# Filters' loop in another order, token tiles in pairs, a fourth bank, and the filters' norms divided out in the second layer's coefficients

## The chip, the cores and the metric

The kernel runs on 1 core of one Trainium2 chip. The time is that of the device, in microseconds (us), the median of several runs. The engines are TensorE (PE, with its weight loads PEld), VectorE (DVE), ScalarE (ACT), GpSimd (POOL) and SyncE (SP), which issues nearly all DMAs.

## The reference

A backbone of two layers over 1024 tokens of width 1024, with 256 context tokens before them. The first layer is attention of two kinds side by side, the second a gated long convolution ("Hyena") of order 2. What the change touches is the second layer's filters and the way their norm is taken:

```
def hyena_filters(L, w1, b1, w2, b2, w3, b3, freq):
    ...                                  # a small MLP over positions, then a decay
    h = h * jnp.exp(-t * jnp.abs(deltas))[:, None, None, :]
    fwd, bwd = h[:, :, 0], h[:, :, 1]
    kern = jnp.concatenate([fwd, zeros, bwd[:0:-1]], axis=0)
    kern = kern / jnp.sum(jnp.abs(kern), axis=0, keepdims=True)
    return jnp.fft.rfft(kern, axis=0)

def long_conv(u, k_f, skip):
    y = irfft(rfft(u, n=2 * L) * k_f)[:, :L]
    return y + u * skip

    u = short_conv(p[..., :3 * 1024], conv_w, conv_b)     # three taps and a bias
    z = parts[0]
    for o in range(2):
        z = parts[o + 1] * long_conv(z, k_f[:, o], skip[o])
```

The first layer's input is `rms_norm(x, w) * (1 + scale) + shift`, token by token.

## The kernel before

The program has stages: the filters' loop (to about 250 us), the first layer's input projections, attention (480 to 990), output projection, and the second layer's projections and convolutions from about 1090 on. PE, ACT, DVE and POOL work each in the order in which the program is written (`manual_schedule`); SP's order is chosen by the framework.

**The filters' loop** (L615) has 38 iterations n. The steps are pairs of a channel block p of 128 channels (8 of them) and a group gq of taps (4), so 32 steps; the second stage runs six iterations behind. In the order of the program one iteration does: `taps` on PE into a two-bank tile `pw`; `second_stage(.., 0)` on PE into a bank of `pq`; `decayed` (L541), the multiplication of the taps by the decay on DVE; two exponentials of the next step on ACT; `spectra(.., 0)`, which takes the second stage out of its bank on DVE, times the reciprocal norm `rns[p]` (L594), into `kc` and stores it to `Kd` in DRAM; `first_stage` of the step before (PE, then a copy `aT` on ACT), twice, with two more exponentials between; `halves`, a sum and a difference on POOL (L561); `norms`, the sum of absolute values on DVE (L548) and its addition on POOL (L552); `second_stage(.., 1)`; once in four the product `pn` with ones (L649), which sums the norm over the partitions; `regroup`, four DMAs `au<-aT`; `spectra(.., 1)`; once in four the reciprocal of the norm (L661). Once in four also `coefs` (three loads) and `split_coefs` (six ACT copies, two POOL and two DVE subtractions, L345 to L349) for the next block.

**Token tiles.** At the end of an iteration generators are advanced: `modulations` (to n = 6), `row_stats` (to n = 11) and `xprep`, for the first layer's input, from n = 11 on, two `yield`s an iteration from n = 13 to 32. `xprep` takes ten tiles of 128 tokens: it scales one by its rows' norm (L408, DVE), loads the next, and for each half of the width transposes four blocks (L414, PE), scales and shifts them in four ACT instructions (L419) into `mraw`, rounds them (L426, DVE, two casts of 128x256 or one of 128x512) and subtracts (L427, POOL).

**Banks.** `pq` hands out the banks t0, t1, v in turn, and c from n = 20 on. A bank is written again only when what it held was read.

**First weights.** At n = 22 (W1N) the first projection weights `w0` are loaded, at n = 24 split into two parts (four ACT copies L678, four POOL subtractions L679), at n = 26 the next ones loaded; products with them are put at n = 32 to 35 (HP) and behind the loop.

**Second layer.** `tables` loads the convolution's coefficients `cw` (L1750, single elements) and tables FA and IA; `kernel_load` loads `Kd` and the skip row, and adds the skip to the spectrum's real part.

## Time and profile before

| | us |
|---|---|
| median of 3 runs | 1794.36 (1793.38 to 1795.69) |
| the profiled execution | 1791.72 |
| its span, first to last instruction | 1789.9 |
| TensorE busy in the span | 1698.6 (95%) |
| VectorE, GpSimd, ScalarE busy | 1136.4, 837.1, 751.7 |

TensorE's matmuls are pipelined, so that their busy times overlap one another and a busy TensorE is not one at its peak. The share of busy time is a mean over stages with different limits, so it is read stage by stage below. The granted clock is that of TensorE, as a share of 2.4 GHz.

### The profile page before, as it was taken

To read this page: it belongs to the slowest core of one execution; us is meant where nothing else is said; L and a number is where in the kernel's file an instruction comes from. 1 tells how busy PE (TensorE), PEld (TensorE's weight loads), DVE (VectorE), ACT (ScalarE), POOL (GpSimd) and SP (SyncE) were. 2 spreads that over 40 slices of the span, in tenths; PEclk is the share of its full clock that TensorE was granted. 3 is DMA by queue.
4 is the path that set the end of the run, shared out by engine and by line. 5 is a ranking of instruction groups with operands and counts; after the bars stand their busy time and mean duration, and the time that the engine had idled before them with its cause. 6 is when DMAs were issued, how large, how long until landed. Compare 5 with 4: busy or idle time off the path is not lost. (4 is left out here: it accounts for less than half of the span.)

```text
span 1789.9 us, 25447 instructions
## 1 busy us (share of the span) xinstructions
PE 1698.6 (95%) x9360; PEld 1313.9 (73%) x9360; DVE 1136.4 (63%) x1625; ACT 751.7 (42%) x1293; POOL 837.1 (47%) x612
## 2 busy tenths in 40 slices
PE   6888899998999999999999999999999999999898
PEld 2555588986766666666666788888888888878786
DVE  6888957636666665466665324556777667756843
ACT  4766621243545545644444333233333333333331
POOL 3667832524179877677777453123222223233300
PEclk8999999999999999999999999999999999999999
DMA  7776787322220010100010226456776666686432
GB/s 258 243 217 200 211 260 266 110 71 72 57 57 28 11 44 14 52 31 24 22 34 22 78 94 161 138 152 203 199 213 174 196 201 196 196 231 181 155 108 104
DMA packets 237372, 236.48 MB, mean 132 GB/s; under 512 B 30575, under 2 KB 195223, under 8 KB 236831
## 3 DMA queue, kind: packets, MB, share of 16 engines
q1 hardware_dynamic: 235072, 232.76, 43.6%
q10 hardware_dynamic: 2176, 2.10, 0.4%
q8 instruction: 74, 1.21, 0.3%
q14 instruction: 50, 0.41, 0.1%
HBM read 152.87 MB, written 61.94 MB: 120 GB/s over the span
## 5 line engine op out<-in xcount | busy, mean ns | idle before, releaser
L1010 DVE TENSOR_REDUCE mx<-pq 128x1 f32<-128x512 f32 x256 | 170.9, 682 | 100.4 <-PE pq L1009 98.6
L1315 ACT ACTIVATE PT<-pw 128x1024 f32<-128x1024 f32 x160 | 163.6, 1025 | 166.1 <-PE pw L1297 160.1
L100 PE MATMUL pw<-h1h,wh 128*128 128x512 f32 x512 | 208.4, 407 | 0.0
L102 PE MATMUL pw<-h1h,wl 128*128 128x512 f32 x512 | 201.3, 393 | 0.0
L101 PE MATMUL pw<-h1l,wh 128*128 128x512 f32 x512 | 200.0, 391 | 0.0
L1209 POOL TENSOR_TENSOR acc<-acc,PT 128x1024 f32<-128x1024 f32 x62 | 147.4, 2378 | 20.4 <-ACT PT L1315 18.9
L1733 POOL TENSOR_TENSOR wl<-wr,wh 128x1024 fp32r<-128x1024 f32 x32 | 77.1, 2409 | 137.8 <-ACT wh L1732 127.5
L102 PEld LDWEIGHTS pw<-h1h,wl 128*128 128x128 f32 x512 | 96.1, 188 | 21.3
L101 PEld LDWEIGHTS pw<-h1l,wh 128*128 128x128 f32 x512 | 96.5, 188 | 17.7
L100 PEld LDWEIGHTS pw<-h1h,wh 128*128 128x128 f32 x512 | 96.5, 188 | 17.4
L1868 POOL TENSOR_TENSOR K<-K,skp 128x512 f32<-128x512 f32 x32 | 42.7, 1337 | 122.7 <-DMA K<-Kd 121.7
L1207 POOL TENSOR_TENSOR acc<-PT,PT 128x1024 f32<-128x1024 f32 x31 | 74.0, 2386 | 52.5 <-ACT PT L1315 49.8
L1881 DVE TENSOR_TENSOR cA<-pq,K 64x512 f32<-64x512 f32 x128 | 88.1, 689 | 1.8
L1877 DVE SCALAR_TENSOR_TENSOR cB<-pq,K 64x512 f32<-64x512 f32 x64 | 44.4, 693 | 70.4 <-PE pq L1874 35.6
L1848 ACT COPY caT<-pq 128x512 f32<-128x512 f32 x64 | 37.6, 588 | 118.1 <-PE pq L102 98.1
L583 PE MATMUL pq<-au,FBk 128*128 128x256 f32 x256 | 71.6, 408 | 14.8 <-DVE kc L594 11.1
L1894 PEld LDWEIGHTS pq<-cA,GB 128*128 128x128 f32 x512 | 67.3, 193 | 15.3 <-issue 10.3
L1200 PE MATMUL pv<-PT,Va 128*64 128x256 f32 x640 | 77.9, 385 | 0.0
L1896 ACT COPY cbT<-pq 128x512 f32<-128x512 f32 x64 | 37.5, 587 | 95.7 <-PE pq L1894 67.1
L1200 PE MATMUL pv<-PT,Vm 128*64 128x256 f32 x640 | 77.7, 385 | 0.0
L1894 PE MATMUL pq<-cA,GB 128*128 128x128 f32 x512 | 68.8, 278 | 7.9 <-DVE cA L1884 6.9
L1911 DVE TENSOR_TENSOR cil<-spare,cih 128x512 fp32r<-128x512 f32 x64 | 53.8, 879 | 34.8 <-ACT cih L1910 34.6
(448 smaller groups left out, 4672.6 us busy)
## 6 DMA issues: line engine op xcount, KB each, us to landing
au<-aT SPq DMA_DIRECT2D x128, 128.0 KB
space<-in_ada_w_dram SPq DMA_DIRECT2D x32, 512.0 KB
wr<-in_hy_w_in_dram SPq DMA_DIRECT2D x32, 512.0 KB
K<-Kd SPq DMA_DIRECT2D x64, 256.0 KB
ad<-caT SPq DMA_DIRECT2D x64, 256.0 KB
cau<-ad SPq DMA_DIRECT2D x32, 512.0 KB
bd<-cbT SPq DMA_DIRECT2D x32, 512.0 KB
spare<-bd SPq DMA_DIRECT2D x64, 256.0 KB
```

Source lines behind the costliest of these rows:

```text
L100: nc.tensor.matmul(ps, lh, rh, start=start, stop=False)
L101: nc.tensor.matmul(ps, lh, rl, start=False, stop=False)
L102: nc.tensor.matmul(ps, ll, rh, start=False, stop=stop)
L583: nc.tensor.matmul(ps[:, i * CB:(i + 1) * CB], FBk[:, 4 * uc + 2 * j + i, :], aus[p, uc][:, 2 * j + i, :], start=True, stop=True)
L1010: nc.vector.reduce_max(m[:, i, j:j + 1], ps, axis=AX.X)
L1200: nc.tensor.matmul(ps[64 * e:64 * e + 64, 0:256], vals[:, 2 * s + j], PT[:, j, 256 * e:256 * e + 256], start=s == 0 and j == 0, stop=s == ...
L1207: eng.tensor_tensor(accs[gi], prev, PT, ALU.add)
L1209: eng.tensor_tensor(accs[gi], accs[gi], PT, ALU.add)
L1315: nc.scalar.activation(PT, ps.rearrange("p (a q) -> p a q", q=512), AF.Exp, scale=SC_A if kind == 0 else SC_M)
L1733: nc.gpsimd.tensor_tensor(wl, f(r), f(wh), ALU.subtract)
L1881: nc.vector.tensor_tensor(A1[64 * e:64 * e + 64], pv[64 * e:64 * e + 64], K[:, 0], ALU.mult)
L1894: nc.tensor.matmul(ps[:, i * P:(i + 1) * P], GB[:, 4 * uc + i, :], A1[:, i, :], start=True, stop=True)
```

## The change

The second copy of a spectrum goes to ScalarE, and both copies no longer multiply. The norm (not its reciprocal) is copied out of its bank by ScalarE and stored to DRAM (`nd`). In the attention (groups 20 and 22) it is loaded again, with a channel on each partition; the skip row is multiplied by it and stored (`sd`), and its reciprocal is taken; in `tables` the short convolution's coefficients of parts 1 and 2 are multiplied by the reciprocal. The convolution then adds the skip times the norm to the unnormalised spectrum, and the part that multiplies the result carries the division.

Token tiles go in pairs: one activation covers 256 columns, one cast and one subtraction 128x512. The four steps of a pair's quarter (transposes; activations; cast and subtraction; at the end of the pair loads and scaling) stand at four places of an iteration: ahead of the taps, behind the decay multiplication, between `halves` and `norms`, and behind `norms`. Five tiles are loaded at once at n = 11, into the three tiles ckh, ckl, kpe as well. As these hold tokens for longer, the weights' load, split and second load move from n = 22, 24, 26 to 26, 32, 34, and the products from n = 32 to 33. The fourth bank joins at the end of n = 6, not 19.

```diff
-W1N = 22
-HP = {32: 1, 33: 1, 34: 1, 35: 1}
+W1N = 26
+XT = ("xt", "xt") + CK + ("xt", "xt", "ckl", "xt", "kpe")
+LN = 2, 1, 2, 0, 0
+HP = {33: 1, 34: 1, 35: 1, 36: 1}
...
-        load()
+        def scaled(t):
+            for i in range(t, min(t + 2, NC + NT)):
+                nc.vector.tensor_scalar(xts[i], xts[i], rr[:, i:i + 1], 0.0, ALU.mult, ALU.add)
+
+        load(5)
         yield
-        for t in range(NC + NT):
+        scaled(0)
+        yield
+        for t in range(0, NC + NT, 2):
...
+            for k0 in range(0, NK, 2):
+                ps = pq()
+                for k in range(2):
+                    for i in range(2):
+                        nc.tensor.transpose(ps[:, (2 * k + i) * P:(2 * k + i + 1) * P], xts[t + i][:, (k0 + k) * P:(k0 + k + 1) * P], ident)
                 yield
...
+                for k in range(2):
+                    kk = k0 + k
+                    nc.scalar.activation(raw[:, k], ps[:, 256 * k:256 * k + 256], AF.Identity, bias=Sh[:, kk:kk + 1], scale=A[:, kk:kk + 1])
                 yield
...
+                nc.vector.tensor_copy(hi, raw)
+                nc.gpsimd.tensor_tensor(lo, raw, f(hi), ALU.subtract)
+                yield
+                if k0 == NK - 2:
+                    load(LN[t // 2])
+                    scaled(t + 2)
+                yield
...
-            nc.vector.tensor_tensor(kc.rearrange("p h u c -> p u h c"), ps.rearrange("p (u h c) -> p u h c", h=2, c=P),
-                                    rns[p].rearrange("p (h c) -> p h c", c=P).unsqueeze(1).to_broadcast([P, 2, 2, P]), ALU.mult)
+            (nc.vector.tensor_copy, nc.scalar.copy)[j](kc.rearrange("p h u c -> p u h c"), ps.rearrange("p (u h c) -> p u h c", h=2, c=P))
...
+            tokens = 12 < n < 33
+            if tokens:
+                pull(toks)
             if 0 < n < N:
                 taps(n)
             if n >= 6:
                 ps0 = second_stage(pb, ub, 0)
             if n < N:
                 decayed(n)
+            if tokens:
+                pull(toks)
...
                 halves(n)
+            if tokens:
+                pull(toks)
+            if n < N:
                 norms(n)
+            if tokens:
+                pull(toks)
...
-                rns[r] = fw.tile([P, CB], F32, tag="rn", bufs=1, name=nm("rn"))
-                nc.vector.reciprocal(rns[r], pn[:, :CB])
+                rn = fw.tile([1, CB], F32, tag="rn", bufs=1, name=nm("rn"))
+                nc.scalar.copy(rn, pn[0:1, :CB])
+                nc.sync.dma_start(nd[:, r, :].unsqueeze(0), rn.rearrange("p (o c) -> p o c", o=2))
...
-            if 12 < n < 33:
-                pull(toks, 2)
-            if n == W1N + 2:
+            if n == W1N + 6:
...
-            if n == W1N + 4:
+            if n == W1N + 8:
...
-            if n == 19:
+            if n == 6:
                 banks.append("c")
...
+        def filter_norms(first):
+
+            if first:
+                nc.sync.dma_start(rc, nd.rearrange("o b c -> c (o b)"))
+                nc.sync.dma_start(sk, I["hy_skip"][0].rearrange("o (b c) -> c (o b)", c=P))
+                return
+            nc.vector.tensor_tensor(sk, sk, rc, ALU.mult)
+            nc.sync.dma_start(sd.rearrange("o b c -> c (o b)"), sk)
+            nc.vector.reciprocal(rc, rc)
...
+                if s == 2 and gi in (20, 22):
+                    filter_norms(gi == 20)
...
+        nc.vector.tensor_tensor(cw[:, :, 8:24], cw[:, :, 8:24], rc.unsqueeze(1).to_broadcast([P, 4, 16]), ALU.mult)
...
-                nc.sync.dma_start(B["skp"], I["hy_skip"][0, o, b * P:(b + 1) * P].partition_broadcast(P))
+                nc.sync.dma_start(B["skp"], sd[o, b].partition_broadcast(P))
```

## Rows read from the trace of the kernel before

**Rows 1.** Busy time by stretch: stretch, length, busy of each engine (instructions), clock, DMA.
```profile
54.31:100.50 46.19, 38.92 (x163) 26.43 (x162) 41.17 (x45) 32.42 (x77) 27.37 (x27) 0.96 0.81 244
100.50:144.56 44.06, 37.02 (x153) 24.53 (x152) 36.69 (x42) 26.77 (x72) 30.00 (x29) 0.92 0.71 212
144.56:223.80 79.24, 68.52 (x297) 47.27 (x297) 72.91 (x86) 50.51 (x138) 62.44 (x66) 0.94 0.69 205
223.80:249.40 25.60, 23.98 (x136) 20.41 (x135) 15.47 (x22) 4.61 (x11) 6.72 (x8) 1.00 0.80 233
480.00:990.00 510.00, 500.23 (x3191) 342.69 (x3191) 316.72 (x537) 258.01 (x360) 383.35 (x216) 1.00 0.10 30
```

**Rows 2.** Waits from 102 to 222 us: who, for whom, total, times, longest.
```profile
ACT dec L536 <- DVE kern L541: 30.2, 14, 3.3
```

**Rows 3.** VectorE in order of time, one iteration: start, length, line, instruction.
```profile
144.56 1.21 DVE L541 TENSOR_TENSOR kern<-pw,dec 128x1024 f32<-128x1024 f32 x1
145.70 0.68 DVE L594 TENSOR_TENSOR kc<-pq,rn 128x512 f32<-128x512 f32 x1
146.29 1.96 DVE L548 TENSOR_REDUCE kabs<-kern 128x256 f32<-128x1024 f32 x1
148.16 0.69 DVE L594 TENSOR_TENSOR kc<-pq,rn 128x512 f32<-128x512 f32 x1
149.21 0.29 DVE L426 CAST h<-mraw 128x256 fp32r<-128x256 f32 x1 [0.36 <-ACT mraw L419]
149.91 0.55 DVE L426 CAST h<-mraw 128x256 fp32r<-128x256 f32 x1 [0.41 <-ACT mraw L419]
150.39 1.21 DVE L541 TENSOR_TENSOR kern<-pw,dec 128x1024 f32<-128x1024 f32 x1
```

**Rows 4.** VectorE's groups from 102 to 222 us: busy, mean ns, idle before.
```profile
L661 DVE RECIPROCAL rn<-pq 128x256 f32<-128x256 f32 x5 | 8.8, 1758 | 0.5
L408 DVE TENSOR_SCALAR xt<-xt,rr 128x1024 f32<-128x1024 f32 x8 | 5.9, 742 | 0.0
L349 DVE TENSOR_TENSOR WB<-b3r,WB 1x256 fp32r<-1x256 f32 x8 | 5.4, 674 | 3.0 <-ACT WB L348 3.0
```

**Rows 5.** GpSimd in order of time, the same iteration, and the weights' split.
```profile
145.92 1.28 POOL L561 TENSOR_TENSOR sum<-kern 128x512 f32<-128x512 f32 x1 [0.69 <-DVE kern L541]
147.15 1.30 POOL L561 TENSOR_TENSOR dif<-kern 128x512 f32<-128x512 f32 x1
...
149.59 0.73 POOL L427 TENSOR_TENSOR h<-mraw,h 128x256 fp32r<-128x256 f32 x1 [0.45 <-DVE h L426]
...
184.52 3.07 POOL L679 TENSOR_TENSOR w<-w,w 128x288 fp32r<-128x288 f32 x4
```

**Rows 6.** TensorE in order of time, one iteration at the full clock.
```profile
219.42 0.66 PE L414 MATMUL pq<-ident,xt 128*128 128x128 f32 x4
219.83 0.36 PE L483 MATMUL pw<-WA,HA 128*128 128x256 f32 x1
...
220.86 1.03 PE L583 MATMUL pq<-au,FBk 128*128 128x256 f32 x4
...
223.44 1.03 PE L583 MATMUL pq<-au,FBk 128*128 128x256 f32 x4
```

**Rows 7.** A group of ScalarE from 102 to 222 us.
```profile
L569 ACT COPY aT<-pq 128x512 f32<-128x512 f32 x36 | 20.5, 568 | 0.1
```

**Rows 8.** DMA issues of SP in order of time: start, length, line.
```profile
182.51 4.21 SPq L578 DMA_DIRECT2D au<-aT  x6
...
1089.81 7.27 SPq L1750 DMA_DIRECT2D cw<-in_hy_conv_w_dram  x3
```

**Rows 9.** Waits of SP's own queue from 30 to 260 us.
```profile
SPq L596 <- DVE kc L594: 29.5, 27, 2.6
```

**Rows 10.** VectorE in order of time, where the second layer's tables arrive.
```profile
1103.02 0.29 DVE L1758 CAST FAh<-tab 128x256 fp32r<-128x256 f32 x1 [3.16 <-DMA tab<-in_FA_dram]
```

**Rows 11.** Waits from 222 to 280 us.
```profile
ACT wh L742 <- DMA Kd<-kc: 17.6, 1, 17.6
```

More of the change, by code (lines that the diff above doesn't have):

```diff
@@ L157, in backbone @@
     Kd = dram.tile([2, NT, P, 2048], F32, tag="Kd", name="Kd")
+    nd = dram.tile([2, NT, P], F32, tag="nd", name="nd")
+    sd = dram.tile([2, NT, P], F32, tag="sd", name="sd")
     zd = dram.tile([NT, P, T], F32, tag="zd", name="zd")
@@ L165, in backbone @@
     nc.vector.memset(ones, 1.0)
+    rc, sk = (cp.tile([P, 16], F32, tag=t, name=t) for t in ("rc", "sk"))
     eps = cp.tile([P, 1], F32, tag="eps", name="eps")
@@ L394, in xprep, with load @@
         xts = []
-        def load():
-            if len(xts) < NC + NT:
-                xt = pre.tile([P, D], F32, tag="xt", bufs=2, name=nm("xt"))
-                nc.sync.dma_start(xt, xsrcs[len(xts)])
+        def load(n_):
+            for t in range(len(xts), min(len(xts) + n_, NC + NT)):
+                tag = XT[t]
+                xt = (pre.tile([P, D], F32, tag=tag, bufs=2, name=nm("xt")) if tag == "xt" else
+                      ckp.tile([P, KEYS], F32, tag=tag, bufs=1, name=nm("xt"))[:, :D])
+                nc.sync.dma_start(xt, xsrcs[t])
@@ L400, in load @@
                 xts.append(xt)
-        load()
+        def scaled(t):
+            for i in range(t, min(t + 2, NC + NT)):
+                nc.vector.tensor_scalar(xts[i], xts[i], rr[:, i:i + 1], 0.0, ALU.mult, ALU.add)
+        load(5)
         yield
-        for t in range(NC + NT):
+        scaled(0)
+        yield
+        for t in range(0, NC + NT, 2):
             who, t0 = ("x", t * P) if t < NC else ("l", (t - NC) * P)
             A, Sh = ada[who, 0, "scale"], ada[who, 0, "shift"]
-            xt = xts[t]
-            nc.vector.tensor_scalar(xt, xt, rr[:, t:t + 1], 0.0, ALU.mult, ALU.add)
-            load()
-            for k0 in (0, 4):
+            for k0 in range(0, NK, 2):
[3 more added lines that the diff above has]
+                        nc.tensor.transpose(ps[:, (2 * k + i) * P:(2 * k + i + 1) * P], xts[t + i][:, (k0 + k) * P:(k0 + k + 1) * P], ident)
@@ L411, in xprep @@
                 yield
-                ps = pq()
-                for i in range(4):
-                    nc.tensor.transpose(ps[:, i * P:(i + 1) * P], xt[:, (k0 + i) * P:(k0 + i + 1) * P], ident)
+                raw = pre.tile([P, 4, P], F32, tag="mraw", bufs=2, name=nm("mraw")).rearrange("p (k i) c -> p k (i c)", k=2)
+                for k in range(2):
+                    kk = k0 + k
+                    nc.scalar.activation(raw[:, k], ps[:, 256 * k:256 * k + 256], AF.Identity, bias=Sh[:, kk:kk + 1], scale=A[:, kk:kk + 1])
@@ L415, in xprep @@
                 yield
-                raw = pre.tile([P, 4, P], F32, tag="mraw", bufs=2, name=nm("mraw"))
-                for i in range(4):
-                    k = k0 + i
-                    nc.scalar.activation(raw[:, i], ps[:, i * P:(i + 1) * P], AF.Identity, bias=Sh[:, k:k + 1], scale=A[:, k:k + 1])
                 if who == "x":
-                    dst = [((hxh[:, k0:k0 + 4, t0:t0 + P], hxl[:, k0:k0 + 4, t0:t0 + P]), raw)]
+                    hi, lo = (x[:, k0:k0 + 2, t0:t0 + 256] for x in (hxh, hxl))
@@ L422, in xprep @@
                 else:
                     th, c = divmod(t0, 512)
-                    dst = [([h0[th, k0 // 2 + j, i][:, :, c:c + P] for i in range(2)], raw[:, 2 * j:2 * j + 2]) for j in range(2)]
-                for (hi, lo), r in dst:
-                    nc.vector.tensor_copy(hi, r)
-                    nc.gpsimd.tensor_tensor(lo, r, f(hi), ALU.subtract)
+                    hi, lo = (h0[th, k0 // 2, i][:, :, c:c + 256] for i in range(2))
+                nc.vector.tensor_copy(hi, raw)
+                nc.gpsimd.tensor_tensor(lo, raw, f(hi), ALU.subtract)
@@ L525, in backbone @@
         fw = fw_es.enter_context(pool("filtw", "right"))
-        aTs, accs, sums, rns, kns, sds, aus = {}, {}, {}, {}, {}, {}, {}
+        aTs, accs, sums, kns, sds, aus = {}, {}, {}, {}, {}, {}
         def decay(n, d):
```

## The prediction

> **What bounds the kernel now.** I read the busy times by stretch first, cut at the starts of the decay multiplication (L541) of the sixth, the fourteenth, the twentieth and the last iteration of the filters' loop (n = 5, 13, 19 and 31) [rows 1]. All edits that can move much lie in this loop. From n = 13 to 31 it takes 44.06 + 79.24 = 123.3 us for 18 iterations: 7.34 each while three banks rotate (to n = 19), 6.60 each after. In the last of these stretches VectorE is busy 72.91 of 79.24 us; TensorE's 68.52 overlaps itself, and its pieces alone take less (below); ScalarE has 50.51 and GpSimd 62.44. Then the waits: ScalarE's exponentials wait for VectorE's multiplication, 30.2 us in 120 [rows 2]. Then one iteration in order of time [rows 3]: from one L541 (144.56) to the next (150.39) VectorE stops only for the casts, which wait 0.36 and 0.41 us for ScalarE. So VectorE sets the period. After the loop (from n = 31) TensorE is busy 23.98 of 25.60 us [rows 1], so a loop that ends sooner moves all that follows forward.
>
> **VectorE's work in the loop.** I count four iterations together, since two token tiles, one norm and one split of coefficients fall into four. Before, four take 4 x 6.60 = 26.4 us. The steps of one iteration, start to start [rows 3]: decay 1.14, spectrum copy 0.59, norm reduction 1.87, second spectrum copy about 0.60, and the casts with their waits 1.6, from 148.76 to 150.39; every second iteration has a scaling of 0.74 besides [rows 4].
>
> What goes: four second copies (to ScalarE), 4 x 0.60 = 2.4; one reciprocal, 1.7 [rows 4]; and of the eight casts of 128x256 four are left of 128x512. One of 256 columns took 0.29 alone [rows 3]; one of 512 costs between that and twice that, and I take 0.40. The remaining first copy loses its multiplication: it reads the same bank in the same shape, so I leave it at 0.59 (a gain of the size of a cast's 0.3 at most, nothing lost). New busy sum of four: 4 x (1.14 + 0.59 + 1.87 + 0.40) = 16.0, two scalings 1.5, two small subtractions of the coefficients 1.3 [rows 4]: **18.8 us**.
>
> **New waits on VectorE.** (a) The casts. They now stand right behind the first spectrum copy, where ScalarE's activations are ready, so the waits of 0.36 and 0.41 go. But GpSimd is then at the sum and difference, which it starts 0.2 after the multiplication ends and which take 1.28 and 1.30 [rows 5]. The second cast of rows 3 started at 149.91 inside a GpSimd subtraction (149.59 to 150.32 [rows 5]) and took 0.55, not 0.29: it came out as that one ended. A cast that is ready 0.59 after the multiplication's end finds about 0.9 of the sum still to run. Bounds 0 and 1.28 (if GpSimd begins the difference first); I take 0.5 each, 2.0 for four, since the sum often starts late behind GpSimd's own queue. The Trainium skill (SBUF — State Buffer, section Who interferes with whom) says that a VectorE copy of this kind and a GpSimd instruction lock each other out, the first to start keeping the port to its end, and that a reduction doesn't take part. The trace agrees in the 0.55 beside 0.29; without that rule the term would be 0 and four iterations 21.4 us, with its worst order 26.5.
>
> (b) The scalings of the next pair now stand at the end of every fourth iteration, and the next instructions of TensorE are that pair's transposes, with the taps of the next iteration queued behind them, and behind those VectorE's next multiplication. So once in four VectorE waits for 0.41 of transposes and 1.03 of taps [rows 6]: 1.4. Before, a whole iteration lay between. (c) The split of coefficients comes behind one more copy in ScalarE's queue; ScalarE's copy of that shape takes 0.57 [rows 7], so VectorE's two subtractions wait about that much more, 0.6 once in four, with 0 and 1.5 as bounds.
>
> Sum: 18.8 + 2.0 + 1.4 + 0.6 = 22.8. I add 0.6 for what a denser loop meets: transfers that land late, and stretches at the lower clock. The granted clock is 0.92 and 0.94 of the full 2.4 GHz in the two token stretches [rows 1], so part of them ran at 1.2 GHz. That gives 23.4 for four, **5.85 us** an iteration; 18 x (6.85 - 5.85) = **18.0 us** gained, for the 18 iterations that took 123.3.
>
> **The others as bounds.** TensorE's pieces: 0.41 transposes, 1.03 taps, and three pieces of 0.86 from 220.86 to 223.44, a fourth behind it [rows 6]: 4.88, four 19.5, plus the norms' product about 0.4. At 0.94 of the clock 21.2. GpSimd: 62.44 - 3.07 (the weights' subtraction that moves, [rows 5]) over 12 iterations is 4.95, and the pairing saves about 0.2 of that: 19.2 for four. ScalarE: 50.51 over 12 is 4.2; the copy adds 0.57, the wider activations give some back. None exceeds 23.4, but all lie within a fifth, so the loop can't go much below 5.1.
>
> **The fourth bank** comes at n = 7, not 20. Its price is the difference of 7.34 and 6.60, 6 x 0.74 = 4.4 us; it is contained in the 18.0, since I set all 18 to one period.
>
> **The loop before the tokens** (n = 5 to 13, 46.19 us): VectorE loses seven second copies and two reciprocals, 4.2 + 3.5 = 7.7. But DMA is busy 0.81 at 244 GB/s [rows 1], so 11.3 MB need at least 46.19 x 0.81 = 37.4. I take 5 of the 7.7 (bounds 0 and 7.7). **Five token tiles at once**: 2.6 MB are asked for at n = 11 where before two loads, 1.05 MB, stood around there. The 1.57 MB more take 5.2 us at 301 GB/s (244/0.81), ahead of the regrouped data that the next second stage reads. I take 4 back (0 to 5.2).
>
> **After the loop.** The first projection weights are now split at n = 32, one step ahead of their use: four GpSimd subtractions, 3.07 [rows 5], hidden before at n = 24. TensorE's first product of them needs all four; the first one comes early, and two pieces of 0.86 of n = 33 cover part. Cost 1.5 (0 to 3.1). The second load of weights moves from n = 26 to 34; ScalarE's first cast of it waited 17.6 us for the last stores of spectra [rows 11], so I take 0 for that.
>
> **The norms in the second layer.** The new instructions on VectorE are a 128x16 product, a 128x16 reciprocal and one product on the convolution's coefficients, some tenths each, in stretches that TensorE bounds. The coefficients' product waits for their load, but VectorE waits there for a table that is loaded behind them (3.16 us until 1103.02 [rows 10]), so 0. The three new transfers move 2048 single elements each. SP took 7.27 for three loads of 3072 single elements [rows 8], so 1.6 each, 4.8 in all; queued behind them are attention's row sums. No row shows a store of that kind. They fall into the attention, where TensorE is busy 500 of 510 us and the DMA engines a tenth of the time [rows 1]; I take 0 (0 to 4.8, if all of it were exposed).
>
> **Sum** against the profiled execution's 1791.72: -18.0 - 5 + 4 + 1.5 = -17.5, 1774.2. The median of the runs is 2.6 above that execution, so **1777 us**.
>
> **Rivals.** *A, the forecast*: 52%. *B, the waits hide*: casts slip in between GpSimd's instructions and nothing but the engines' sums counts; 5.1 an iteration, -31.5 - 6 + 4 + 0.5 = -33: 1761. For it: ScalarE and the buffers leave room for TensorE to run ahead, as it does now. Against: once in four the chain (b) has no slack. 20%. *C, the waits are worse*: the casts always wait the full 0.9 of the sum (1.6 more for four), and TensorE's stops cost another 0.6 at the lower clock; 25.6 for four, 6.4 an iteration, 18 x 0.45 = 8: -8 - 4 + 5 + 2 = -5: 1789. For it: the sum starts right behind the multiplication when GpSimd is idle; against: GpSimd is nearly full and will often start later. 21%. *D, slower: the queue of transfers is the bound*. SP issues four loads, two stores and about one more in an iteration; six issues took 4.21 where the queue was loaded, 0.70 each [rows 8]. If issues go to 0.95, seven take 6.7 and the loop gains nothing, while the burst and the weights' split cost 5.5: 1800. Decides from about 0.9 an issue; against it speaks that SP itself waited 29.5 us for VectorE's copies [rows 9]. 5%. Something else 2%.
>
> **Range.** B's end to C's end with the bounds of the burst and the split: 1763 to 1789. A measurement tells about 0.2%, 3.6 us, from no change: faster takes A, B and over half of C, 0.84; same 0.10; slower 0.06.
>
> **What would show it.** Iterations from n = 13 on of 5.6 to 6.1 us; a stop of 1.4 of VectorE behind every fourth iteration, released by the taps; casts of 0.7 to 1.2 where they now take 0.3 to 0.55; a pause near n = 12 with loads of tokens in flight; a stop of TensorE before the first product. Wrong it would be if the period stays over 6.5, if the casts keep 0.4, or if attention or the convolutions change length.

## The result and the profile after

The changed kernel takes **1802.38 us** (median of 13 runs, 1797.67 to 1805.76) against 1791.93 (13 runs of the kernel before beside it): ratio 1.0058, interval 1.0044 to 1.0071. It is slower by 0.6%, where 1777 was forecast. Its profiled execution took 1797.67, its span 1795.8; that of before 1791.72. So this trace shows 5.9 of the 10.4 us between the medians.

The stretches of [rows 1], cut at the same multiplications (L557 now; stretch, length, busy of each engine with instructions, clock, DMA share, GB/s), in the changed kernel:

```profile
54.53:106.02 51.49, 38.36 (x164) 26.73 (x164) 33.55 (x38) 37.63 (x88) 27.31 (x27) 0.97 0.85 245
106.02:145.13 39.11, 34.70 (x156) 24.74 (x154) 32.12 (x31) 27.10 (x68) 28.97 (x26) 0.95 0.68 196
145.13:225.18 80.05, 67.16 (x290) 48.51 (x290) 63.40 (x58) 50.58 (x124) 56.38 (x50) 0.87 0.62 184
225.18:253.57 28.39, 25.82 (x137) 21.18 (x136) 9.76 (x12) 8.95 (x18) 10.16 (x11) 1.00 0.88 238
484.00:994.00 510.00, 499.97 (x3188) 342.35 (x3188) 317.12 (x539) 257.89 (x360) 382.98 (x216) 1.00 0.10 30
```

Iterations 5 to 13 take 5.3 us more, 13 to 19 take 5.0 less, 19 to 31 take 0.8 more. From iteration 31 to the first product of the weights' part `wh` with the tokens' `h` it is 2.7 more, from there to the second layer's first short convolution (`u<-pw,cw`) 851.4 us against 851.3, and from there to the end 1.7 more. VectorE lost 9.5 us of busy time in the longest stretch (72.91 to 63.40) and the stretch did not get shorter; what fell with it is the granted clock, 0.94 to 0.87. The attention is the same to 0.3 us in TensorE's busy time.

Where VectorE's time went, its instructions in order of time at the end of a pair of tiles (start, length, line), in the changed kernel:

```profile
149.92 1.21 DVE L557 TENSOR_TENSOR kern<-pw,dec 128x1024 f32<-128x1024 f32 x1
151.05 0.68 DVE L610 COPY kc<-pq 128x512 f32<-128x512 f32 x1
151.65 1.18 DVE L437 CAST h<-mraw 128x512 fp32r<-128x512 f32 x1
152.74 1.92 DVE L564 TENSOR_REDUCE kabs<-kern 128x256 f32<-128x1024 f32 x1
154.59 1.79 DVE L412 TENSOR_SCALAR xt<-xt,rr 128x1024 f32<-128x1024 f32 x2
159.19 1.23 DVE L557 TENSOR_TENSOR kern<-pw,dec 128x1024 f32<-128x1024 f32 x1 [2.80 <-PE pw L500]
160.80 0.69 DVE L610 COPY kc<-pq 128x512 f32<-128x512 f32 x1 [0.38 <-PE pq L599]
161.41 0.42 DVE L437 CAST h<-mraw 128x512 fp32r<-128x512 f32 x1
```

And TensorE's over the same time:

```profile
150.98 1.03 PE L599 MATMUL pq<-au,FBk 128*128 128x256 f32 x4
155.87 1.47 PE L425 MATMUL pq<-ident,xt 128*128 128x128 f32 x4 [3.87 <-DVE xt L412]
157.00 0.56 PE L499 MATMUL pw<-WA,HA 128*128 128x256 f32 x1
158.85 1.91 PE L599 MATMUL pq<-au,FBk 128*128 128x256 f32 x4
```

The iteration from 149.92 to 159.19 is 9.3 us long; the next three are 6.4, 6.8 and 4.8, and this period repeats. VectorE scales the next pair (to 156.4), and TensorE, which has nothing else it may start, waits 3.87 us for that. It then runs at half the clock: the transposes take 1.47 instead of 0.66 [rows 6], the second stage 1.91 instead of 1.03. So VectorE's 2.80 of waiting is only the first part; the stretches show the rest (same columns, the iteration ahead, the stop, and the iteration behind it):

```profile
145.13:149.90 4.77, 4.47 (x23) 3.26 (x23) 4.77 (x4) 3.85 (x10) 4.62 (x5) 1.00 0.60 166
149.90:159.19 9.29, 5.30 (x20) 3.87 (x19) 6.49 (x7) 3.87 (x10) 5.17 (x5) 0.74 0.86 255
159.19:165.60 6.41, 6.41 (x28) 4.72 (x27) 4.18 (x5) 4.20 (x10) 3.64 (x3) 0.85 0.44 142
```

The full clock, 2.4 GHz, in the iteration ahead; 0.74 of it across the stop, 0.85 behind it.

### The profile page after: what moved, and what is told of

Its sections match the earlier page's. It is cut to its first block, busy times and chain, and to the rows that moved or that the text cites. A ratio compares the mean times of both kernels' runs of the same rounds, so it can differ in the third digit from the quotient of the medians.

```text
span 1795.8 us, 25376 instructions
## 1 busy us (share of the span) xinstructions
PE 1697.4 (95%) x9360; PEld 1317.0 (73%) x9360; DVE 1108.8 (62%) x1572; ACT 761.6 (42%) x1293; POOL 833.9 (46%) x596
## 5 line engine op out<-in xcount | busy, mean ns | idle before, releaser
L1769 POOL TENSOR_TENSOR wl<-wr,wh 128x1024 fp32r<-128x1024 f32 x32 | 76.6, 2393 | 135.1 <-ACT wh L1768 111.8
L1931 PEld LDWEIGHTS pq<-cA,GB 128*128 128x128 f32 x512 | 67.5, 193 | 15.1 <-issue 10.2
L1948 DVE TENSOR_TENSOR cil<-spare,cih 128x512 fp32r<-128x512 f32 x64 | 53.1, 867 | 36.6 <-ACT cih L1947 34.7
```

The source lines that it names most:

```text
L1769: nc.gpsimd.tensor_tensor(wl, f(r), f(wh), ALU.subtract)
L1931: nc.tensor.matmul(ps[:, i * P:(i + 1) * P], GB[:, 4 * uc + i, :], A1[:, i, :], start=True, stop=True)
```

## The experiments

Lengths of the stages in each profiled execution, in us, and the medians. The last stage, the tail, runs from iteration 31 to the first product of the weights' part `wh` (the second weights, rounded) with the tokens' `h`, `pw<-wh,h` in the trace. Each ratio is against runs of the kernel before on the same chip; where a kernel was built a second time (e18), its ratio came out 0.0025 higher, so ratios that are closer than that don't rank two kernels.

| kernel | 5-11 | 11-13 | 13-19 | 19-31 | 31-wh | median | ratio (interval) |
|---|---|---|---|---|---|---|---|
| before | 36.0 | 10.2 | 44.1 | 79.2 | 31.7 | 1791.9 | |
| after | 36.6 | 14.9 | 39.1 | 80.1 | 34.4 | 1802.4 | 1.0058 (1.0044-1.0071) |
| e18_after_again | 42.7 | 13.6 | 41.0 | 80.5 | 34.3 | 1804.9 | 1.0083 (1.0062-1.0104) |
| e1_scale_early | 40.7 | 13.6 | 40.0 | 70.5 | 35.1 | 1794.2 | 1.0014 (1.0002-1.0025) |
| e2_norms_only | 35.1 | 10.2 | 45.0 | 82.7 | 31.1 | 1799.3 | 1.0037 (1.0023-1.0050) |
| e7_copies_vector | 37.7 | 10.2 | 43.8 | 79.7 | 32.2 | 1792.1 | 0.9999 (0.9986-1.0011) |
| e3_bank_only | 35.9 | 10.1 | 42.7 | 78.2 | 31.7 | 1792.7 | 1.0000 (0.9990-1.0010) |
| e4_tokens_only | 36.5 | 13.6 | 42.5 | 83.9 | 36.4 | 1807.0 | 1.0081 (1.0068-1.0094) |
| e5_gate | 37.5 | 13.6 | 41.0 | 76.6 | 34.6 | 1798.1 | 1.0031 (1.0017-1.0044) |
| e12_front | 36.8 | 13.7 | 45.9 | 70.5 | 33.7 | 1796.5 | 1.0032 (1.0020-1.0044) |
| e16_three_fewer | 37.1 | 13.7 | 40.3 | 73.3 | 34.7 | 1789.1 | 0.9985 (0.9972-0.9998) |
| e15_store_act | 36.8 | 15.7 | 38.0 | 69.6 | 34.8 | 1792.2 | 0.9997 (0.9982-1.0012) |
| e19_late_first | 37.7 | 12.7 | 42.8 | 71.3 | 35.4 | 1794.9 | 1.0010 (0.9997-1.0023) |
| e8_tail_vector | 43.5 | 13.6 | 40.8 | 69.9 | 34.2 | 1794.7 | 1.0017 (1.0001-1.0033) |
| e13_w1_early | 39.3 | 13.6 | 40.4 | 70.1 | 33.5 | 1793.7 | 1.0009 (0.9997-1.0021) |
| e11_spread | 37.2 | 13.7 | 44.5 | 76.8 | 33.2 | 1800.5 | 1.0044 (1.0028-1.0060) |
| e14_all | 39.5 | 13.6 | 47.7 | 70.5 | 35.6 | 1798.9 | 1.0046 (1.0029-1.0064) |
| e17_best | 36.9 | 15.3 | 37.9 | 69.4 | 34.1 | 1792.7 | 0.9999 (0.9983-1.0016) |
| e20_late_first_tail | 37.5 | 12.2 | 43.6 | 69.3 | 34.7 | 1794.9 | 1.0018 (1.0000-1.0035) |

### The stop at each pair: e1_scale_early

```diff
+                if k0 == NK - 4:
+                    scaled(t + 2)
                 if k0 == NK - 2:
                     load(LN[t // 2])
-                    scaled(t + 2)
```

> The changed kernel with one edit: the scaling of the next pair of token tiles stands one iteration earlier (third quarter of a pair instead of the last); loads stay. In the changed kernel's trace every fourth iteration takes 9.2 us, TensorE stands 3.9 us before the pair's first transposes and VectorE 2.8 us behind it. Theory S (the chain scaling, transposes, taps, next multiplication stops both engines): the fourth iteration falls to about 6.3, the period of four from 27.2 to about 24.3, four such places, so 10 to 13 us less than the changed kernel: ratio to before about 0.998 to 1.001. Rival P (VectorE's casts and scalings standing behind GpSimd's instructions are what the loop lost): the casts still take 1.2 to 1.5, the period stays over 26.5, under 4 us less.

1794.2: 8.2 us less than the changed kernel, by one scaling moved an iteration ahead; 10 to 13 were expected. Iterations 19 to 31 fall from 80.1 to 70.5, and the clock there is 0.98:

```profile
149.70:220.20 70.50, 61.94 (x291) 43.62 (x290) 65.26 (x58) 49.95 (x124) 57.91 (x50) 0.98 0.70 209
```

70.5/3 is 23.5 us for four iterations. The casts stay long (1.15 us on average, 14 of them in 145 to 225 us), so rival P is out. In this loop VectorE is indeed the fullest engine, busy 65.26 of 70.50. The forecast had 23.4, but that the two agree is luck: its sum held 1.4 for a stop that e1 doesn't have, and put VectorE's busy time for four at 18.8 + 2.0 = 20.8, where 65.26/3 is 21.8; the waits it set too high make up for it. Nor does it hold for iterations 13 to 19, which take 40.0 us in e1, 6.7 each: there 13 and 17 take 6.7 and 8.0, at 0.80 and 0.70 of the clock, while 21, 25 and 29, at the same place of later pairs, take 4.7 to 5.8. Behind the loop and ahead of it some of the gain is lost, which the next experiments follow.

### The norms alone: e2_norms_only and e7_copies_vector

In the kernel before, only the norms' part of the change:

```diff
-            nc.vector.tensor_tensor(kc..., ps..., rns[p]...to_broadcast([P, 2, 2, P]), ALU.mult)
+            (nc.vector.tensor_copy, nc.scalar.copy)[j](kc..., ps...)
...
-                nc.vector.reciprocal(rns[r], pn[:, :CB])
+                nc.scalar.copy(rn, pn[0:1, :CB])
```

> The kernel before with the norms' part alone: spectra are copied (first by VectorE, second by ScalarE) and not multiplied, the norm goes to DRAM and is applied in the second layer; order of the loop, single token tiles and the bank at n = 20 stay. If VectorE sets the period of the old loop, four iterations lose 2.4 + 1.7 of 26.4: 6.6 falls to 5.7 or less, 15 to 20 us for the loop with tokens, and some for the part before: ratio 0.988 to 0.992. Rival: another engine or the transfers stand right behind VectorE, or the second layer's added transfers cost what the loop gains: ratio 0.997 or more. The second layer's stage is read apart: from the first short convolution to the end it should take within 1 us of before.

1799.3, slower by 0.37%: a miss in the sign. Iterations 19 to 31 grow from 79.2 to 82.7 although VectorE is busy 60.97 us there instead of 72.91 [rows 1]:

```profile
145.60:228.30 82.70, 68.93 (x299) 48.38 (x298) 60.97 (x71) 57.17 (x153) 62.46 (x66) 0.92 0.68 200
```

In the waits of the stretch from 145 to 230 us (who, for whom, total, times, longest), first the kernel before, then e2:

```profile
DVE h L426 <- ACT mraw L419: 4.5, 13, 0.6
```

```profile
DVE h L429 <- ACT mraw L422: 17.4, 24, 2.1
PEld pq L586 <- ACT mraw L422: 5.9, 4, 2.9
```

VectorE's casts now wait for ScalarE's activations, as ScalarE's new copy (0.59) stands in its queue ahead of them. To test this, e7 is e2 with both copies on VectorE:

```diff
-            (nc.vector.tensor_copy, nc.scalar.copy)[j](kc..., ps...)
+            nc.vector.tensor_copy(kc..., ps...)
```

> The kernel before with the division by the norms moved to the second layer, as in e2_norms_only (1799.34), but with both K copies of an iteration on VectorE instead of one on each engine. A copy costs VectorE 0.68 us, as the product before did (0.67), so VectorE has what it had before, less a reciprocal of 1.8-2.0 us in four iterations; ScalarE is as before. Theory C (the loop is a chain through ScalarE: the K copy of 0.59 us stands ahead of the four activations of 1.5 us, and casts, GpSimd's differences and the next transposes follow them; VectorE waits for them 17.4 us in e2 against 4.5 before): iterations 19 to 31 come back from 82.7 to 76-80 us and the whole to 1788-1793. Rival (it is the norms' small copy and its store on SyncE's queue, or a bank freed later): iterations 19 to 31 stay at 81-83.5 and the whole at 1797-1801.

1792.1 and 79.7 us: as before. VectorE's casts wait 7.4 us in 145 to 225, where they waited 16.0 in e2 and 4.5 before. So the copy on ScalarE is the price (7 us), and the reciprocals, one in four iterations, that e7 still saves bring nothing: VectorE is busy 70.02 us there, 2.9 less than before, and the stretch is 0.5 longer. Less work on VectorE alone thus doesn't shorten the old loop, and more on ScalarE lengthens it. I read this as a ring through TensorE (transposes), ScalarE (activations) and VectorE (casts) that is about as long as VectorE's work; that is inferred from the waits, and no run opens the ring.

### The other two parts alone: e3_bank_only and e4_tokens_only

```diff
-            if n == 19:
+            if n == 6:
                 banks.append("c")
```

> The kernel before with the fourth bank in turn from n = 7 instead of 20, nothing else. If the six iterations from n = 13 to 19 were 0.74 us longer than the later ones for want of a bank: 4 us less there (44.1 to about 40), ratio 0.997 to 0.999. Rival: the first tokens are slower for another reason (whole casts, a colder clock): under 1.5 us.

1792.7, no change; 13 to 19 falls by 1.4 us, not by 4.4. So of the difference of 7.34 and 6.60 us an iteration at most a third was the bank's.

e4 is the changed kernel with the old copies, products with the reciprocal on VectorE and all:

```diff
-            (nc.vector.tensor_copy, nc.scalar.copy)[j](kc..., ps...)
+            nc.vector.tensor_tensor(kc..., ps..., rns[p]...to_broadcast([P, 2, 2, P]), ALU.mult)
```

> The changed kernel without the norms' part: spectra multiplied by the reciprocal norm on VectorE as before, nothing added to the second layer; pairs of tiles, the new order, the bank and the loads as in the changed kernel. Theory S: VectorE stands on the chain in every fourth iteration, and its work grows by 0.6 an iteration and 1.7 once in four: the period of four grows from 27.2 to 30 or more, 15 to 25 us slower than the changed kernel, ratio to before 1.013 to 1.020. Rival (TensorE's stops alone set the period, VectorE has room in them): within 5 us of the changed kernel. If it equals the kernel before or beats it, the norms' part is what costs.

1807.0, within 5 us of the changed kernel, as the rival had it; the period of four grows to 83.9/3 = 28.0, not to 30. The token tiles' new order with the bank costs 15 us against before. What the norms' part brings there is at the edge of what the ratios tell (1.0081 against 1.0058, and 1.0083 in e18); in iterations 19 to 31 it is 3.4 to 3.8 us. Where the order is old, it costs 7.4 in the median.

### The front: e18_after_again, e5_gate, e12_front, e16_three_fewer, e15_store_act, e19_late_first

SyncE's issues in the changed kernel (start, length), among them three token loads some ten iterations ahead of their place in the program:

```profile
44.73 0.38 SPq L407 DMA_DIRECT2D xt<-in_x_dram  x1
47.67 0.33 SPq L385 DMA_DIRECT2D xs<-in_x_dram  x1
48.69 1.14 SPq L407 DMA_DIRECT2D xt<-in_x_dram  x2
51.84 0.33 SPq L385 DMA_DIRECT2D xs<-in_x_dram  x1
...
92.30 0.59 SPq L407 DMA_DIRECT2D xt<-in_ctx_dram  x1
95.57 0.46 SPq L407 DMA_DIRECT2D xt<-in_ctx_dram  x1
```

I took them for the cause of the longer front. e5 is e1 with a one-column write ahead of each load into a key tile, which holds it at its place:

```diff
+                if tag != "xt":
+                    nc.gpsimd.memset(xt[:, 0:1], 0.0)
                 nc.sync.dma_start(xt, xsrcs[t])
```

> The changed kernel with the next pair's scaling one iteration earlier (e1_scale_early, 1794.2), and with a one-column memset on GpSimd ahead of each token load into the key tiles. In e1 three of those loads are issued at 45.87 and 49.83 us, in the middle of the statistics' loads, although the program asks for them ten iterations later; the memset holds them at their place in the program. Theory H (the loads pulled forward take the transfers' time from the filters' own regrouped loads, `PE pq L600 <- DMA au<-aT` 7.0 us in 54:106): iterations 5 to 13 go from 54.3 to 45-48 us and the whole to 1785-1789. Rival Q (the K copies' split between VectorE and ScalarE makes SyncE issue the four regrouped loads in one bunch behind a K store): iterations 5 to 13 stay at 51-54 and the whole at 1792-1796. If the five loads in a row at iteration 11 only move the burst, iterations 11 to 13 grow by 3-6 us and the whole is 1789-1793.

1798.1, worse than e1. The loads in the later pairs got the write too, and two iterations there (22 and 26) take 11.4 and 11.2 us instead of 7.2 and 6.8 in e1; so the whole doesn't decide. Iterations 5 to 13 take 51.1, in rival Q's range. e12 holds the three loads only and spreads them:

```diff
+                if 1 < t < 5:
+                    nc.gpsimd.memset(xt[:, 0:1], 0.0)
...
-        load(5)
+        load(2)
...
+                if t == 0 and k0 < NK - 2:
+                    load(1)
```

> e1_scale_early (1794.2) with the three token loads into the key tiles held back by a one-column memset, those three loads alone, and asked for one in an iteration from n = 13 on. e5_gate held every load into a key tile, and its later memsets put 4.7 us stretches into the loop (iterations of 11.4 us). Theory H as it now stands (iterations 5 to 13 are bound by transfers: 11.1 to 11.3 MB at 235 to 246 GB/s take 45.3 to 47.9 us where the token loads come later, 12.1 to 12.9 MB take 50 to 57 where three of them are pulled in; a load is 0.52 MB, so 2.1 us): iterations 5 to 13 move 11.2 MB in 46-50 us, 13 to 19 take 41-44 instead of 40, 19 to 31 stay at 70-71, and the whole is 1788-1792. Rival (a chain, not the transfers' sum: the copies of the first stage, their four regrouped loads and the product of the next block's first group, which waits for them in the iteration after a short one): iterations 5 to 13 stay at 51-55 although the megabytes fall, and the whole is 1792-1797.

1796.5, in the rival's range. Iterations 5 to 13 take 50.5, between the two ranges; 19 to 31 are intact (70.5), 13 to 19 take 45.9 instead of 40.0, 11 to 13 are as long as ever. e16 leaves out these loads altogether, so that three token tiles are zeros and its output is another:

```diff
+                if 1 < t < 5:
+                    nc.gpsimd.memset(xt, 0.0)
+                else:
+                    nc.sync.dma_start(xt, xsrcs[t])
```

> e1_scale_early (1794.2) without the three early token loads: the three key tiles of the first burst are set to zero by GpSimd at iteration 11 instead of being loaded, so three token tiles enter the projections as zeros. 1.57 MB (three of 0.52) are then moved by nobody. Theory M (iterations 5 to 19 are bound by the transfers' sum: holding the three loads back in e12_front gave 50.5 instead of 54.3 in iterations 5 to 13 and took 45.9 instead of 40.0 in 13 to 19): at 240 GB/s 1.57 MB are 6.5 us, so 5 to 13 fall from 51-57 to 46-49, 13 to 19 stay at 39-41, and the whole is 1786-1790. Rival (the waits of the next block's first product for its regrouped loads on SyncE's queue, which e15_store_act took away, set it, not the sum): 5 to 13 stay at 50-55 and the whole at 1792-1796.

1789.1, 5 us under e1, but the stage in question takes 37.1 + 13.7 = 50.8, as in e12, not the 46 to 49 forecast. So the early loads are not what lengthens it. Nor do the 5 us show as transfers saved in the loop: in the profiled executions iterations 5 to 31 take 164.5 us against 164.8 in e1, and 3.2 of the 4.7 us between the two lie in the first projections (from the first to the last product of `wh` with `h` 115.5 instead of 118.7), where the changed kernel's two executions also differ, 116.2 and 118.8.

The table shows where it does grow, once the stage is cut at iteration 11. Iterations 5 to 11 take 35.1 to 37.7 us in the kernel before and in most others, with VectorE relieved (24.45 us busy in e2) or not (31.85 before). In five executions they take 39.3 to 43.5. e18 is the changed kernel once more:

> The changed kernel once more, unaltered: its profiled execution was the fastest of its thirteen (1797.67 against a median of 1802.38), so its trace shows 5.9 of the 10.4 us that the medians are apart. If the rest lies in the same places (a longer stop at each pair, or a front of 55-57 us instead of 51.5, as e1 and e8 differ by 3 us there with the same instructions), an execution of about 1802 shows stages 5 to 13 or 19 to 31 longer by 3-6 us. Rival: it lies behind the loop, in the projections or the second layer, as low clock.

1804.66 in this execution: the first theory holds for the most part; its span is 7.0 us longer than the other's, iterations 5 to 11 are 6.1 longer and the whole loop from 5 to 31 is 7.1; behind it, it loses 2.6 in the first projections and gains as much back in the second layer. TensorE in order of time, e18:

```profile
81.23 1.03 PE L599 MATMUL pq<-au,FBk 128*128 128x256 f32 x4
82.10 0.59 PE L674 MATMUL pq<-kabs,ones 128*128 128x256 f32 x2
87.08 2.05 PE L599 MATMUL pq<-au,FBk 128*128 128x256 f32 x4 [3.44 <-DMA au<-aT]
88.91 1.91 PE L584 MATMUL pq<-sum,FKc 128*128 128x512 f32 x2
```

and SyncE's issues there:

```profile
80.54 0.43 SPq L385 DMA_DIRECT2D xs<-in_x_dram  x1
81.08 0.38 SPq L611 DMA_DIRECT2D Kd<-kc  x1
81.56 2.61 SPq L594 DMA_DIRECT2D au<-aT  x4
84.27 0.54 SPq L611 DMA_DIRECT2D Kd<-kc  x1
```

Iteration 9, at 4.8 us where the kernel before takes 7.6, is over before the four regrouped loads issued from 81.56 on have landed; TensorE stands 3.44 us, falls to half the clock, and iteration 10 takes 13.4. In the first execution of the same kernel iteration 9 takes 4.8 too, TensorE stands 2.50, the product behind it takes 1.10, so the clock has held, and iteration 10 takes 9.5. That is 3.9 of the 6.1 us. But such a stop does not mark out the five: e5 and e12 have longer ones at the same place, 4.32 and 4.16 us with the clock falling, and take 37.5 and 36.8 from 5 to 11. What makes these five longer stays open. In e15 ScalarE stores the copy that it makes itself, so that these loads no longer stand behind that store:

```diff
-            (nc.scalar if tail else nc.sync).dma_start(Kd[...], kc...)
+            (nc.scalar if tail or j else nc.sync).dma_start(Kd[...], kc...)
```

> e1_scale_early (1794.2) with the store of the K copy that ScalarE makes issued by ScalarE itself, right behind its copy, instead of by SyncE. SyncE's queue waits for that copy now (4.4 us in 54:106) with the regrouped loads behind it. Theory Q (SyncE's in-order queue delays the regrouped loads, `PE pq L600 <- DMA au<-aT`): the product's waits fall to under 3 us in that window, iterations 5 to 13 go from 54.3 to 48-51 us, and the whole to 1788-1792. Rival (0.4-0.6 us of issuing in front of the activations on ScalarE, in a loop whose chain runs through it): iterations 19 to 31 grow from 70.5 to 74-78 and the whole is 1796-1802.

The product's waits for these loads fall from 7.0 to 2.8 us, as expected, and 19 to 31 doesn't grow; the whole is 1792.2. But 5 to 11 is 36.8, the usual length: now the copies wait for their buffers' stores instead, 10.7 us where it was 3.6 in e1 (54 to 108 us, e15):

```profile
DVE kc L611 <- DMA Kd<-kc: 6.5, 4, 2.5
PE pq L425 <- DVE xt L412: 6.4, 1, 6.4
ACT kc L611 <- DMA Kd<-kc: 4.2, 2, 2.5
```

The second line is the other part of the front. Iterations 11 to 13 take 10.1 to 10.2 us in all four kernels with the old order of the token tiles and 12.2 to 15.7 in all others. There the first pair is scaled, directly ahead of its transposes, and that stop of 4.3 to 6.4 us no kernel of the kind of e1 removes. e19, built on e15, puts the first transposes one place later (the yields at the pair's end, which let it catch up, are left out here):

```diff
         scaled(0)
         yield
+        yield
```

> e15_store_act (1792.15) with one change: the first pair's transposes stand behind the taps and the second stage of iteration 13 instead of in front of them, one place later in the iteration, and the pair catches up at its end. Theory S1 (the first pair has the same stop as the others had, since its scaling at the end of iteration 12 stands directly ahead of its transposes; iterations 11 to 13 take 13.6 to 15.7 us in every kernel with the paired order, whatever its transfers, and 10.1 to 10.2 in the four with the old one): iterations 11 to 13 fall from 15.7 to 10-12 us, 13 to 19 stay at 38-39, and the whole is 1787-1790. Rival (those iterations wait for transfers, or the stop only moves to the place behind the taps): 11 to 13 at 13.5-15.5, or 13 to 19 longer by what they gain, and the whole 1791-1794.

1794.9. Iterations 11 to 13 fall from 15.7 to 12.7, but 13 to 19 grow from 38.0 to 42.8: the rival. TensorE's wait for the scaling falls from 6.43 to 1.47 us, and two others come up, 2.81 and 2.88, for VectorE's copies out of a bank.

### The tail: e8_tail_vector and e13_w1_early

```diff
-            (nc.vector.tensor_copy, nc.scalar.copy)[j](kc..., ps...)
+            (nc.vector.tensor_copy if tail or j == 0 else nc.scalar.copy)(kc..., ps...)
```

> e1_scale_early (1794.2) with both K copies of the last block on VectorE, so that ScalarE, whose queue issues that block's K stores, has no copy to do between them. Theory T (ScalarE's in-order queue: its copies wait behind the stores it issues, one of which takes 5.33 us for a buffer, and VectorE's copies then wait 13.6 us for those stores): from iteration 31 to the first product with the split rest of the weights 35.1 goes to 31-33 us and the whole to 1790-1792. Rival (SyncE's queue with eleven regrouped loads, and the weights' second half loaded at 242 us instead of before the loop's end, hold the tail): it stays at 34-35.5 and the whole at 1793-1796.

The tail is 34.2 instead of 35.1 and the whole unchanged: the rival's numbers. In e8 ScalarE's split waits for the load of the weights' second half, which stands at 244.27 behind eleven regrouped loads, where before (W1N + 4 = 26) it came within the loop and the split waited for ScalarE's own stores [rows 11]:

```profile
244.27 1.23 SPq L707 DMA_DIRECT2D w<-in_w_in_dram  x1
...
251.21 1.44 ACT L767 CAST wh<-w 128x288 fp32r<-128x288 f32 x4 [14.59 <-DMA w<-in_w_in_dram]
```

e13 asks for that half earlier:

```diff
                     for uc in range(1, 4):
                         regroup(NT - 1, uc)
+                        if uc == 1:
+                            w1 = ...
+                            nc.sync.dma_start(w1, win[:, 4:8, 0:288])
```

> e8_tail_vector (1794.7) with the weights' second half asked for between the regrouped loads of the last block, ahead of the last eight of them instead of behind all. In e8 ScalarE's split of that half waits 14.59 us for that load (issued at 244.27 us, the split starts at 251.21). Theory W (that load's place on SyncE's queue holds the tail once the K copies are off ScalarE): from iteration 31 to the first product with the split weights 34.2 goes to 30.5-32.5 us, and the whole to 1790-1792.5. Rival (the K stores, eight on ScalarE's queue and 13.35 us long in e8, end last anyway): 33.5-35 us and the whole at 1794-1796.

```profile
231.85 1.01 SPq L685 DMA_DIRECT2D w<-in_w_in_dram  x1
...
232.67 13.14 ACTq L612 DMA_DIRECT2D Kd<-kc  x8
245.85 1.44 ACT L767 CAST wh<-w 128x288 fp32r<-128x288 f32 x4 [14.05 <-DMA Kd<-kc]
```

The load no longer ends last, the stores of ScalarE's queue do: 33.5 us, 0.7 less than e8.

But ScalarE's long wait is not what the tail is made of. TensorE is busy through nearly all of it, in the kernel before and in the changed one (same columns as the stretches above):

```profile
223.80:255.50 31.70, 29.89 (x175) 25.72 (x174) 15.47 (x22) 6.79 (x17) 11.22 (x14) 1.00 0.80 225
225.20:259.60 34.40, 31.75 (x178) 26.70 (x177) 9.74 (x12) 10.72 (x23) 13.23 (x15) 1.00 0.89 233
```

and its waits there in the changed kernel are

```profile
PE pq L102 <- DVE kc L610: 1.0, 1, 1.0
PE pq L599 <- DMA au<-aT: 0.8, 1, 0.8
PE pq L599 <- ACT w L702: 0.8, 2, 0.6
```

None is for `wh`, nor is one in e1, e8 or e13. Of the 2.7 us that the changed kernel's tail is longer, 1.9 is work, mainly four more products of the first stage that the new order leaves behind the start of iteration 31, and 1.0 is waits (2.6 against 1.6 before). What e8 and e13 shorten is the first of these lines: one of VectorE's last copies, which itself waits for a store to free its buffer. TensorE waits for it 2.0 us in e1, 1.1 in e8 and not at all in e13. These are single executions; in the medians none of it can be told from nothing.

### Together: e11_spread, e14_all, e17_best, e20_late_first_tail

> All three together: the earlier scaling, the loads into the key tiles held at their place by a memset and asked for one in an iteration instead of five at once (two at iteration 11, one each at 12, 13 and 14), and the last block's K copies on VectorE. If the three losses are separate: iterations 5 to 13 at 45-47 us, 19 to 31 at 70-72, from iteration 31 to the split weights 31-33, and the whole at 1780-1785, under the kernel before (1791.9). Rival (what is gained ahead of the products is waited for there, since the weights and the K stores come no earlier): the loop is shorter by as much but the tail longer, and the whole is 1787-1792.

1800.5; it has e5's write in the later pairs (19 to 31: 76.8).

> e12_front and e13_w1_early together. If both theories hold: iterations 5 to 13 46-50 us, 19 to 31 70-71, the tail 30.5-32.5, the whole 1784-1789, under the kernel before (1792). If the losses only move: 1790-1795.

1798.9: e12's longer 13 to 19 (47.7), and a tail of 35.6.

> What paid, together: the earlier scaling (e1_scale_early, -8 us), ScalarE issuing the store of its own copy (e15_store_act, 1792.15), the last block's copies on VectorE with the weights' second half asked for earlier (e13_w1_early, tail 33.5 instead of 35.1), and the first pair's scaling ahead of iteration 12's reduction, so that the first transposes, which wait 4.3 to 6.4 us for it, wait 2 us less. If the parts add up: iterations 5 to 13 at 49-51 us, 19 to 31 at 69-70, tail 33-34, the whole 1786-1790. If what is gained in the loop is waited for behind it: 1791-1793.

1792.7. The profiled execution took 1785.06, with iteration 31 reached 9.9 us earlier than before, but the median equals that of before: its runs go from 1785 to 1799, and no trace shows where the slower ones lose it.

> e19_late_first with the last block's K copies on VectorE and the weights' second half asked for earlier, as in e13_w1_early (where the tail was 33.5 instead of 35.1 us and the whole 0.5 less than e1's). If the parts add up: the tail 33-34 us and the whole 0.5-2 us under e19, 1785.5-1789.5, under the kernel before (1792) by more than 0.15%. If the tail's gain is waited for behind it: as e19, within 1 us.

1794.9, as e19. No version that computes everything is measurably faster than the kernel before.

## Why the prediction was wrong, step by step

In the profiled executions the forecast was -17.5 us and the outcome +5.9. Iterations 13 to 31 were to give 18.0 and gave 4.1; 5 to 13 were to give 1 and cost 5.3; the tail was to cost 1.5 and cost 2.7; the rest was set at 0 and cost 2.0, all but 0.3 of it behind the second layer's first short convolution. The medians are 10.4 apart, so 4.5 more are not in that trace. The 2.6 that were added for the median were not there either: over 13 runs the kernel before takes 1791.93, not 1794.36.

- **Term (b), the scalings ahead of the transposes, 1.4: the step that failed most.** The mechanism was right and the size wrong. It was worked out with durations at the full clock [rows 6] and counted VectorE's wait alone. TensorE stands 3.87 us, and what follows runs at 1.2 GHz for some 5 us more; the first stage takes 1.02 again from 161.71 on. VectorE waits 2.80. Four iterations take 26.7 us in the changed kernel and 23.5 in e1, so the stop costs 3.2, and e1 gives back 8.2 us of the whole. Rival C had this stop at the lower clock, at 0.6.
- **"So VectorE sets the period."** Wrong for the kernel before. e2 takes 12 us of VectorE's work out of 19 to 31 and that stretch grows by 3.5. The rows read there [rows 2, 3] showed VectorE busy, but its two waits of 0.36 and 0.41 for ScalarE in that iteration were the sign that other engines were as tight.
- **The sum of 23.4 us for four iterations.** e1's 23.5 meets it by luck. The casts (a) were 1.18, 0.42, 1.48 and 1.28 in the changed kernel's period, 4.4 us for four, and 4.6 in e1, where 4 x 0.40 + 2.0 = 3.6 was set; the two scalings took 2.25 in e1 where 1.5 was set; and (b), 1.4 in the sum, is gone there. A cast that starts inside GpSimd's sum or difference comes out 0.3 us behind that one's end (151.65 to 152.83 in the changed kernel, the sum ending at 152.54), while 0.42 is the one that ran alone. By the Trainium skill (SBUF — State Buffer, section Who interferes with whom) the engine that starts first keeps the shared port to the end of its instruction; the trace agrees. And one period was set for all 18 iterations: 13 to 19 take 39.1 in the changed kernel and 40.0 in e1, not 35.1.
- **The fourth bank, 4.4 us.** 1.4 in its stretch, nothing in the whole (e3).
- **Iterations 5 to 13, -5 and +4.** The relief is worth under 1 us (e2: 45.3 instead of 46.2); iterations 5 to 11 take 35 to 38 us in most executions whatever VectorE has to do. The burst was not where I put it: SyncE's order, which the framework chooses, pulled three of the five loads to 45 to 49 us. They were not the price either (e12, e16). What costs is the first pair's stop, which the forecast left out: iterations 11 to 13 are 3.4 to 5.5 us longer with it (4.7 in the changed kernel). e19 could move this stop but not remove it, so that its cause is the scaling's place alone is not shown. In five executions 5 to 11 is longer as well, for a reason that stays open.
- **After the loop, +1.5.** It is 2.7, of which 1.9 is TensorE's work that now lies behind the start of iteration 31, and 1.0 waits. 0.8 of the waits come as ScalarE splits the first weights, inside the bounds set for that split. The second load's place, set at 0, holds ScalarE in e8, but no wait of TensorE for it shows in any of these executions.
- **The norms in the second layer, 0.** Nothing contradicts it: from the first to the last short convolution (`u<-pw,cw`) 542.1 us before, 544.1 after, 541.4 in e18, 542.4 in e7, which has this part.
- **Rival D** had the sign, with another mechanism. SyncE's issues in the loop stayed at 0.61 to 0.65 us (2.46 for four in the changed kernel's first execution, 2.61 in e18), far from the 0.9 that it needed.
- **The range.** Rival B's own sum is 1761, just outside the 1763 that was called its end.

What stays open: what sets the length of iterations 5 to 11 (waits for regrouped loads and for stores replace each other there while the transfers run at 216 to 260 GB/s) and makes it 39 to 44 us in five executions; what lowers the clock in 13 to 19 of e1; and why e17's gain in the loop isn't in its median.

## What to carry to other kernels

Before counting an engine's relief as time, look for the short waits between its neighbours: work moved from the fullest engine to the next one can make a loop longer, as in e2. Work that is placed directly ahead of its reader on another engine costs more than its own length if TensorE stands for it, since TensorE came back at half the clock here; moving such work one iteration ahead was worth 8 us. A long wait of another engine, like ScalarE's 14 us in the tail, is no loss where TensorE has work and doesn't wait for what comes of it. And a reordered program must be read again on the queue that someone else orders.

## What the runs showed of the hardware

- After the stops of 3.4 to 3.9 us shown here TensorE's granted clock is at its lower level: transposes 1.47 instead of 0.66, the first stage 1.91 instead of 1.02, second-stage products 1.91 to 2.05 instead of 1.03, while in e1's iterations 19 to 31, where no wait is over 1.9, the stretch kept 0.98 of the clock. The length of a stop doesn't tell the level by itself: behind 2.50 us (changed kernel) and 3.15 us (e13) the product took 1.10 and 1.19, behind 2.64 us (e18) 2.05.
- VectorE's scalings of a pair took 1.42 for two with GpSimd idle (e15, first pair), 1.79 beside one GpSimd subtraction (the changed kernel) and 2.25 beside two GpSimd instructions (e1): the same work, up to 0.8 us apart.
- A copy out of a bank cost VectorE what a product with another operand did: 0.68 us each for 128x512 (on average, changed kernel and kernel before). Leaving the multiplication out saved nothing.
